# Hand-overs of a three-layer network on one core: norms' powers, weight splits, blanking and interleaving moved between engines and places

## The chip, the core and the metric

One core of one Trainium2 chip runs the whole program. The metric is device microseconds of one execution; a kernel's time is the median of its runs. TensorE (PE) does the matrix products, VectorE (DVE) and GpSimd (POOL) elementwise work, ScalarE (ACT) activations and copies, SyncE (SP) issues the transfers; PEld is PE's loading of stationary operands.

## The reference

A sequence of 512 tokens with 1024 features passes three residual layers, all in fp32: first a mixer (an RWKV-like scan beside a pooling branch) and the PEER layer, a lookup of 16 of 16384 experts in each of 8 heads; then a layer with an even mixer (latent and differential attention) and a gated convolutional FFN; then one with an odd mixer (dilated and stick-breaking attention) and another FFN. Around every mixer and FFN of the last two layers there are norms of this kind:

```python
def rms_norm(x, g):
    xf = x.astype(jnp.float32)
    y = xf * lax.rsqrt(jnp.mean(xf * xf, axis=-1, keepdims=True) + NORM_EPS)
    return (y * g.astype(jnp.float32)).astype(x.dtype)

h = conv_ffn(rms_norm(x, ffn_pre_g[i]), ffn_w_up[i], ffn_conv_w[i], ffn_conv_b[i], ffn_w_down[i])
x = x + rms_norm(h, ffn_post_g[i])
```

The first layer ends with one norm more (`norm_f`), whose output is the residual of what follows.

## The kernel before

**Products.** The 512 tokens are four tiles `t` of 128. Every fp32 product is made of three (`mm3`, lines 114 to 119): both operands are split into a rounded part and the rest, `hi` and `lo`, and hi·hi, hi·lo and lo·hi are summed in one PSUM bank. `K.unit` (58 to 68) fetches a weight tile of 128x1024 through the SP queue, lets ScalarE round it to `whi` (line 64) and subtracts to get `wlo` (line 67), on GpSimd and VectorE in turn unless an engine is named. The raw tile and each half have three buffers.

**Hand-overs.** At the end of a mixer or an FFN each token tile is normalised, added to the residual `st.x` and normalised again for the next layer. `square` (198) sums the squares of one half of 512 columns on ScalarE while it leaves PSUM; `add` (202) multiplies both halves by the gain on VectorE (208), calls `total`, and adds to the residual (211); `feed` (162) sums the squares of the new residual (169), calls `total`, and `lay` (179) scales by power and gain (185, VectorE), transposes on PE (190), copies to `hhi` (192, ScalarE) and subtracts to `hlo` (193, VectorE). `total` (173) adds the half sums and the epsilon on VectorE (176) and raises to -1/2 on GpSimd (177):

```python
nc.vector.scalar_tensor_tensor(out=r, in0=r, scalar=float(eps), in1=ms[:, 1:2], op0=ALU.add, op1=ALU.add)
nc.gpsimd.tensor_tensor(out=r, in0=r, in1=self.k.mhalf[:, 0:1], op=ALU.pow)
```

`Stream.project` (214) makes the next layer's first three units for columns 0 to 255 (tiles 0 and 1), then for the rest, so it starts once two tiles are laid. `project_out` (305) is a mixer's output projection for two token tiles; it is a generator that yields after each weight unit, and the last three units are taken tile by tile. `finished` (840) drives it and does the tile's hand-over when it is complete. In `ffn` (234) the last three units of the down projection are taken tile by tile as well; the first half of the output columns is kept in `y0` (287).

**The PEER end.** Tokens 0 to 127 do not go through the dense expert product: `chosen` (596) gathers their 256 expert rows by indirect transfers that GpSimd issues (619), with four row buffers, and VectorE folds each in (626, 635). The other 384 tokens meet all 128 expert units in `dense` (555): an up unit and a down unit each. `interleave` (2034) deals steps of a second generator between the steps of a first: after step i of `n_main` it has done `(i + 1) * n_fill // n_main`. Two gather steps go beside each of the first 26 dense units; from then on line 712 deals the rest, chained with `end` for tile 0, over 92 units. `end` (723) sums squares (735), yields, works out two powers on GpSimd (740 to 744) and lays the tile; for tile 0 the transposes are queued behind the last down matmul put down so far (`self.mark`), and they take the PSUM banks of the up products. Tiles 1 to 3 follow after the last down products.

**Order.** A scheduler orders each engine's instructions by readiness and by place in the program, so a later instruction can stand before an earlier one where nothing binds it. `issue_after` binds an instruction behind a given one on its engine. ScalarE evaluates its functions from loaded tables (ACT_TABLE_LOAD); `exp_ln` (70) loads the one that has both exp and ln.

**The odd mixer.** The query tiles are kept with one half of the partitions blank, so that two heads can share a key tile; `blank` (863) clears them on GpSimd before the first projection, and `apart` (856) fills the rest. In both mixers the last attention (`diff`, `dilated`) runs its token blocks 1 and 0, then blocks 3 and 2 with `finished` for tiles 0 and 1 in between, and then `finished` for tiles 2 and 3.

Of the kernel before, what the change touches and what calls it, by code (L numbers as in the profile page):

```python
# [135 lines left out]
class Stream:  # L136
# [25 lines left out]
    def feed(self, t, gain, pool):  # L162

        k, nc = self.k, self.k.nc
        ms = k.small.tile([128, 2], F32, name=k.name("ms"), tag="fms", bufs=4)
        y = pool.tile([128, D], F32, name=k.name("xn"), tag="xn", bufs=2)
        for h in range(2):
            sl = slice(h * 512, (h + 1) * 512)
            nc.scalar.activation(y[:, sl], self.x[:, t, sl], AF.Square, scale=1.0 / 32.0, accum_out=ms[:, h:h + 1])
        self.total(ms, 1e-6)  # L170
        self.lay(t, self.x[:, t, :], y, ms[:, 0:1], gain, lambda: self.bank("feed", (128, 4, 128)))

    def total(self, ms, eps):

        nc, r = self.k.nc, ms[:, 0:1]
        nc.vector.scalar_tensor_tensor(out=r, in0=r, scalar=float(eps), in1=ms[:, 1:2], op0=ALU.add, op1=ALU.add)
        nc.gpsimd.tensor_tensor(out=r, in0=r, in1=self.k.mhalf[:, 0:1], op=ALU.pow)

    def lay(self, t, x, y, r, gain, psum):

        k, nc = self.k, self.k.nc
        cols = slice(t * 128, (t + 1) * 128)
        for h in range(2):
            sl = slice(h * 512, (h + 1) * 512)
            nc.vector.scalar_tensor_tensor(out=y[:, sl], in0=x[:, sl], scalar=r, in1=gain[:, sl],  # L185
                                           op0=ALU.mult, op1=ALU.mult)
            p = psum()
            for i in range(4):
                c = 4 * h + i
                nc.tensor.transpose(p[:, i, :], y[:, c * 128:(c + 1) * 128], k.ident)  # L190
            hi, lo = self.hhi[:, 4 * h:4 * h + 4, cols], self.hlo[:, 4 * h:4 * h + 4, cols]
            nc.scalar.copy(hi, p)
            nc.vector.tensor_tensor(out=lo, in0=p, in1=hi, op=ALU.subtract)  # L193
# [8 lines left out]
    def add(self, t, halves, ms, gain, pool):  # L202
# [3 lines left out]
        cuts = [slice(h * 512, (h + 1) * 512) for h in range(2)]  # L206
        for h, sl in enumerate(cuts):
            V.tensor_tensor(out=y[:, sl], in0=halves[h], in1=gain[:, sl], op=ALU.mult)  # L208
        self.total(ms, 1e-6)
        for sl in cuts:  # L210
            V.scalar_tensor_tensor(out=self.x[:, t, sl], in0=y[:, sl], scalar=ms[:, 0:1], in1=self.x[:, t, sl],  # L211
# [22 lines left out]
def ffn(k, st, a, li, pre, out=None):  # L234
# [3 lines left out]
    with ExitStack() as ctx:  # L238
# [7 lines left out]
        with open_pool(tc, name=k.name("ffn_w"), bufs=2) as work:  # L246
# [10 lines left out]
            early = st.project([k.unit(a[f"ffn_up{li}"][i]) for i in range(3)], "up")  # L257
            for f in range(NF):
# [7 lines left out]
                V.tensor_tensor(out=alo[:, f, :], in0=us[0], in1=ahi[:, f, :], op=ALU.subtract)  # L266
        tail = ctx.enter_context(open_pool(tc, name=k.name("ffn_t"), bufs=1))
# [17 lines left out]
        for t in range(NT):  # L285
            st.square(acc[t], ms[t], 0, tail)
            A.copy(y0[:, t, :], acc[t])
# [6 lines left out]
        for t in range(NT):  # L294
# [3 lines left out]
            st.add(t, (y0[:, t, :], acc[t]), ms[t], gpost, tail)  # L298
# [6 lines left out]
def project_out(k, st, ohi, olo, w, toks):  # L305
# [9 lines left out]
    for c in range(n - 3):  # L315
        wt = k.unit(w[c])
# [3 lines left out]
    ws = [k.unit(w[c]) for c in range(n - 3, n)]  # L320
# [79 lines left out]
class Peer:  # L400
# [242 lines left out]
    def run(self, x, free_x, dram, ctx2, pre, ps, tag):  # L643
# [9 lines left out]
        with ExitStack() as ctx, ExitStack() as gctx, ExitStack() as ectx:  # L653
# [57 lines left out]
            with open_pool(tc, name="pe_gc", bufs=2) as self.gpool:  # L711
                interleave(dense, 118 - EARLY, chained(fill, self.end(st, 0, acc, g, gpre, tail, ps)), 258)
            rctx.close()
            run_all(self.last(gctx.enter_context(open_pool(tc, name="pe_last", bufs=1, side="right"))))
            tail = ctx.enter_context(open_pool(tc, name="pe_t2", bufs=2))
            for t in range(1, NT):
# [6 lines left out]
    def end(self, st, t, u, g, gpre, pool, ps):  # L723
# [13 lines left out]
        for _ in range(1 + 6 * (t == 0)):  # L737
            yield
        s = ms[:, :, 2]
        G.tensor_tensor(out=s, in0=ms[:, :, 0], in1=ms[:, :, 1], op=ALU.add)  # L740
        G.tensor_scalar(out=s[:, 0:1], in0=s[:, 0:1], scalar1=1e-5, scalar2=None, op0=ALU.add)
        G.tensor_scalar(out=ms[:, 0, 3:4], in0=s[:, 0:1], scalar1=1e-6, scalar2=None, op0=ALU.mult)
        G.tensor_tensor(out=s[:, 1:2], in0=s[:, 1:2], in1=ms[:, 0, 3:4], op=ALU.add)
        G.tensor_tensor(out=s, in0=s, in1=k.mhalf[:, 0:2], op=ALU.pow)
# [111 lines left out]
def apart(k, dst, src):  # L856


    k.nc.scalar.copy(dst[0][HALF[0]], src[HALF[0]])
    k.nc.vector.tensor_copy(dst[1][HALF[1]], src[HALF[1]])  # L860


def blank(k, pairs):
    for z in range(2):
        for pair in pairs:
            k.nc.gpsimd.memset(pair[z][HALF[1 - z]], 0.0)
# [6 lines left out]
def even(k, st, a, pre):  # L873
# [3 lines left out]
    with ExitStack() as ctx:  # L877
# [14 lines left out]
        k.exp_ln()  # L892
# [169 lines left out]
        run_all(at.pipeline([diff(h, i) for i in (1, 0) for h in range(4)], 2))  # L1062
        fill = finished(k, st, project_out(k, st, ohi, olo, wo, (0, 1)), gpost, gpre, tail)
        interleave(at.pipeline([diff(h, i) for i in (3, 2) for h in range(4)], 2), 8, fill, 14)
# [3 lines left out]
def odd(k, st, a, pre):  # L1068
# [3 lines left out]
    with ExitStack() as ctx:  # L1072
# [11 lines left out]
        blank(k, qs)  # L1084
        k.exp_ln()
# [3 lines left out]
        def proj(fs):  # L1089
            for f in fs:  # L1090
                p = st.project1(k.unit(a["od_in"][f]), "pj")
                if f < 6:
                    apart(k, qs[f], p)
# [24 lines left out]
        with open_pool(tc, name="od_st", bufs=2) as wk:  # L1118
# [48 lines left out]
            for y, p in zip((sq[0], sk[0], sq[1]), st.project([k.unit(a["od_in"][f]) for f in (12, 14, 13)], "lr")):  # L1167
                apart(k, y, p) if isinstance(y, list) else A.copy(y, p)
            A.copy(sk[1], st.project1(k.unit(a["od_in"][15]), "pj"))
# [55 lines left out]
        run_all(at.pipeline([dilated(hs, i) for i in (1, 0) for hs in (2, 3)], 2))  # L1225
        fill = finished(k, st, project_out(k, st, ohi, olo, wo, (0, 1)), gpost, gpre, tail)
        interleave(at.pipeline([dilated(hs, i) for i in (3, 2) for hs in (2, 3)], 2), 4, fill, 10)
# [932 lines left out]
```

## Time and profile before

| | |
|---|---|
| median of 3 runs | 3101.58 us (3099.12 to 3106.04) |
| the profiled execution's own time | 3105.84 us |
| its span, first to last instruction | 3104.1 us |
| mean granted clock of TensorE | 0.981 |
| PE, DVE, ACT, POOL busy | 95%, 65%, 44%, 25% |

The profile is of one execution. Times are microseconds from the start of its span, durations of groups nanoseconds. A row of a timeline gives start, duration, engine, line, operation, output and inputs by the program's names; in square brackets stands the idle time before it and what ended it. An engine that is held up inside an instruction shows as busy. The granted clock (PEclk) is TensorE's share of full speed, 1.00 for 2.4 GHz and 0.50 for 1.2.

### The profile page before, as it was taken

To read this page: it belongs to the slowest core of one execution; us is meant where nothing else is said; L and a number is where in the kernel's file an instruction comes from. 1 tells how busy PE (TensorE), PEld (TensorE's weight loads), DVE (VectorE), ACT (ScalarE), POOL (GpSimd) and SP (SyncE) were. 2 spreads that over 40 slices of the span, in tenths; PEclk is the share of its full clock that TensorE was granted. 3 is DMA by queue.
4 is the path that set the end of the run, shared out by engine and by line. 5 is a ranking of instruction groups with operands and counts; after the bars stand their busy time and mean duration, and the time that the engine had idled before them with its cause. 6 is when DMAs were issued, how large, how long until landed. Compare 5 with 4: busy or idle time off the path is not lost. (4 is left out here: it accounts for less than half of the span.)

```text
span 3104.1 us, 45731 instructions
## 1 busy us (share of the span) xinstructions
PE 2952.8 (95%) x17602; PEld 2493.7 (80%) x17602; DVE 2027.9 (65%) x3939; ACT 1359.3 (44%) x2483; POOL 768.8 (25%) x540
## 2 busy tenths in 40 slices
PE   7888999997899999999998999989999899999999
PEld 5666669997789999999997977668888777888887
DVE  6777668999987887888886446665551444655522
ACT  5444353357533333333333355564442354544422
POOL 0000015610014444444441022122222331122222
PEclk9999999999999999999999999899999999999999
DMA  2001152343348999999995432222332242133322
GB/s 91 27 20 33 62 182 97 102 147 153 146 151 315 335 331 345 321 337 336 332 336 210 140 101 82 89 96 96 99 98 94 79 136 91 52 100 99 95 95 82
DMA packets 176201, 476.07 MB, mean 153 GB/s; under 512 B 18768, under 2 KB 68688, under 8 KB 175728
## 3 DMA queue, kind: packets, MB, share of 16 engines
q1 hardware_dynamic: 139120, 338.93, 32.5%
q0 software_dynamic: 36864, 134.23, 11.8%
q8 instruction: 138, 2.26, 0.3%
q14 instruction: 79, 0.65, 0.1%
HBM read 448.59 MB, written 24.51 MB: 152 GB/s over the span
## 5 line engine op out<-in xcount | busy, mean ns | idle before, releaser
L64 ACT CAST whi<-raw 128x1024 fp32r<-128x1024 f32 x494 | 518.5, 1051 | 713.9 <-PE pu L118 190.7
L67 DVE TENSOR_TENSOR wlo<-raw,whi 128x1024 fp32r<-128x1024 f32 x366 | 457.6, 1251 | 462.4 <-ACT whi L64 453.6
L67 POOL TENSOR_TENSOR wlo<-raw,whi 128x1024 fp32r<-128x1024 f32 x128 | 310.8, 2430 | 1081.0 <-ACT whi L64 988.1
L117 PE MATMUL pu<-pe_hhi,whi 128*128 128x384 f32 x1024 | 349.6, 341 | 2.3 <-ACT gl L545 1.8
L119 PE MATMUL pu<-pe_hhi,wlo 128*128 128x384 f32 x1024 | 348.0, 340 | 0.0
L118 PE MATMUL pu<-pe_hlo,whi 128*128 128x384 f32 x1024 | 347.8, 340 | 0.0
L118 PE MATMUL pacc<-wlo,ahi 128*128 128x512 f32 x768 | 302.7, 395 | 0.0
L117 PE MATMUL pacc<-whi,ahi 128*128 128x512 f32 x768 | 294.1, 395 | 3.1 <-ACT ahi L590 3.1
L119 PE MATMUL pacc<-whi,alo 128*128 128x512 f32 x768 | 290.7, 398 | 3.3 <-DVE alo L591 3.3
L119 PE MATMUL up<-res_h,wlo 128*128 128x512 f32 (+1 forms) x752 | 283.1, 377 | 1.0 <-DVE wlo L67 1.0
L118 PE MATMUL up<-res_h,whi 128*128 128x512 f32 (+1 forms) x752 | 283.6, 377 | 0.0
L117 PE MATMUL up<-res_h,whi 128*128 128x512 f32 (+1 forms) x752 | 283.4, 378 | 0.1
L253 DVE SCALAR_TENSOR_TENSOR u<-up,ffn_par,u 128x511 f32<-128x511 f32 (+1 forms) x176 | 131.5, 748 | 142.8 <-ACT u L251 139.7
L619 POOL DMA_INDIRECT row<-pe_rows,pe_gs x128 | 166.0, 1297 | 195.9 <-DVE pe_gs L626 174.2
L619 POOL DMA_INDIRECT row<-pe_v,pe_gs x128 | 164.8, 1287 | 196.1 <-DVE pe_acc L635 186.0
L117 PEld LDWEIGHTS pu<-pe_hhi,whi 128*128 128x128 f32 x1024 | 193.4, 189 | 7.6 <-ACT gl L545 2.1
L118 PEld LDWEIGHTS pu<-pe_hlo,whi 128*128 128x128 f32 x1024 | 193.4, 189 | 4.1
L119 PEld LDWEIGHTS pu<-pe_hhi,wlo 128*128 128x128 f32 x1024 | 193.1, 189 | 0.5
L119 PEld LDWEIGHTS pacc<-whi,alo 128*128 128x128 f32 x768 | 145.0, 189 | 38.1 <-DVE alo L591 3.8
L117 PEld LDWEIGHTS pacc<-whi,ahi 128*128 128x128 f32 x768 | 144.3, 188 | 33.1 <-ACT ahi L590 3.8
L118 PEld LDWEIGHTS pacc<-wlo,ahi 128*128 128x128 f32 x768 | 144.3, 188 | 30.9
L635 DVE SCALAR_TENSOR_TENSOR pe_acc<-row,pe_gs,pe_acc 128x1024 f32<-128x1024 f32 x128 | 163.9, 1280 | 2.8 <-DMA row<-pe_v,pe_gs 2.3
(502 smaller groups left out, 6295.2 us busy)
## 6 DMA issues: line engine op xcount, KB each, us to landing
raw<-pe_u SPq DMA_DIRECT2D x128, 512.0 KB
raw<-pe_v SPq DMA_DIRECT2D x128, 512.0 KB
raw<-ffn_up SPq DMA_DIRECT2D x88, 512.0 KB
raw<-ffn_dn SPq DMA_DIRECT2D x44, 512.0 KB
pe_gd<-go SPq DMA_DIRECT2D x24, 784.0 KB
gc<-pe_gd SPq DMA_DIRECT2D x12, 1536.0 KB
mraw<-mx_in SPq DMA_DIRECT2D x80, 128.0 KB
raw<-pe_wq SPq DMA_DIRECT2D x16, 512.0 KB
```

The costliest lines, as they stand in the source:

```text
L64: nc.scalar.copy(hi, raw)
L67: eng.tensor_tensor(out=lo, in0=raw, in1=hi, op=ALU.subtract)
L117: mm(out, l[0], r[0], start=first, stop=False)
L118: mm(out, l[0], r[1], start=False, stop=False)
L119: return mm(out, l[1], r[0], start=False, stop=last)
L253: V.scalar_tensor_tensor(out=u[:, d:], in0=p[:, :S - d], scalar=par[:, o + 2 - d:o + 3 - d], in1=u[:, d:], op0=ALU.mult, op1=ALU.add)
L619: G.indirect_dma_start(out=r, out_offset=None, in_=table[z], in_offset=bass.IndirectOffsetOnAxis(ap=idx[:, j:j + 1], axis=0))
L635: V.scalar_tensor_tensor(out=acc, in0=row("v", j), scalar=w[:, j:j + 1], in1=acc, op0=ALU.mult, op1=ALU.add)
```

## The change

- `total` adds the epsilon to the first half's sum on VectorE, and ScalarE makes the power: Ln of the second sum with the first as bias, then Exp at scale -0.5. The tables for both are loaded after the FFN's up projection and after the last dense unit; the loads in `even` and `odd` go.
- `end` works out its sums on VectorE; for tiles 1 to 3 the power is Ln and Exp, for tile 0 it stays on GpSimd. Tile 0 yields 17 times before its power instead of 7, and 268 steps are dealt instead of 258.
- The weight splits of the FFN's first three units, of `project_out` and of the odd mixer's first four units are all on VectorE.
- In the FFN the first half of the output is multiplied by the gain on its way into `y0`, by VectorE, instead of copied by ScalarE.
- `apart` clears the blank halves on VectorE, queued behind the last `lo` of `lay`; `blank` goes.
- Four steps (in `odd` three) of `finished` are dealt into token blocks 1 and 0 of the last attention.

```diff
     def feed(self, t, gain, pool):
-        ms = k.small.tile([128, 2], F32, name=k.name("ms"), tag="fms", bufs=4)
+        ms = k.small.tile([128, 4], F32, name=k.name("ms"), tag="fms", bufs=4)
         for h in range(2):
-        self.total(ms, 1e-6)
-        self.lay(t, self.x[:, t, :], y, ms[:, 0:1], gain, lambda: self.bank("feed", (128, 4, 128)))
+        r = self.total(ms, 1e-6)
+        self.lay(t, self.x[:, t, :], y, r, gain, lambda: self.bank("feed", (128, 4, 128)))
     def total(self, ms, eps):
-        nc, r = self.k.nc, ms[:, 0:1]
-        nc.vector.scalar_tensor_tensor(out=r, in0=r, scalar=float(eps), in1=ms[:, 1:2], op0=ALU.add, op1=ALU.add)
-        nc.gpsimd.tensor_tensor(out=r, in0=r, in1=self.k.mhalf[:, 0:1], op=ALU.pow)
+        nc, r = self.k.nc, ms[:, 2:3]
+        nc.vector.tensor_scalar(out=ms[:, 0:1], in0=ms[:, 0:1], scalar1=float(eps), scalar2=None, op0=ALU.add)
+        nc.scalar.activation(r, ms[:, 1:2], AF.Ln, bias=ms[:, 0:1])
+        nc.scalar.activation(r, r, AF.Exp, scale=-0.5)
+        return r
     def lay(self, t, x, y, r, gain, psum):
...
-            nc.vector.tensor_tensor(out=lo, in0=p, in1=hi, op=ALU.subtract)
+            self.laid = nc.vector.tensor_tensor(out=lo, in0=p, in1=hi, op=ALU.subtract).ins
     def sums(self):
...
-    def add(self, t, halves, ms, gain, pool):
+    def add(self, t, halves, ms, gain, pool, y0=None):
+        ys = [y[:, sl] for sl in cuts]
+        if y0 is not None:
+            ys[0] = y0
         for h, sl in enumerate(cuts):
-            V.tensor_tensor(out=y[:, sl], in0=halves[h], in1=gain[:, sl], op=ALU.mult)
-        self.total(ms, 1e-6)
-        for sl in cuts:
-            V.scalar_tensor_tensor(out=self.x[:, t, sl], in0=y[:, sl], scalar=ms[:, 0:1], in1=self.x[:, t, sl],
+            if h or y0 is None:
+                V.tensor_tensor(out=ys[h], in0=halves[h], in1=gain[:, sl], op=ALU.mult)
+        r = self.total(ms, 1e-6)
+        for h, sl in enumerate(cuts):
+            V.scalar_tensor_tensor(out=self.x[:, t, sl], in0=ys[h], scalar=r, in1=self.x[:, t, sl],
     def project(self, units, bank):
...
-            early = st.project([k.unit(a[f"ffn_up{li}"][i]) for i in range(3)], "up")
+            early = st.project([k.unit(a[f"ffn_up{li}"][i], V) for i in range(3)], "up")
             for f in range(NF):
                 for i in (2 * f, 2 * f + 1):
...
+        k.exp_ln()
...
         for t in range(NT):
-            A.copy(y0[:, t, :], acc[t])
+            V.tensor_tensor(out=y0[:, t, :], in0=acc[t], in1=gpost[:, 0:512], op=ALU.mult)
         for f2 in range(n - 3):
...
             for i, w in enumerate(ws):
-            st.add(t, (y0[:, t, :], acc[t]), ms[t], gpost, tail)
+            st.add(t, (None, acc[t]), ms[t], gpost, tail, y0[:, t, :])
             if out is None:
...
     for c in range(n - 3):
-        wt = k.unit(w[c])
+        wt = k.unit(w[c], k.nc.vector)
         for t in toks:
-    ws = [k.unit(w[c]) for c in range(n - 3, n)]
+    ws = [k.unit(w[c], k.nc.vector) for c in range(n - 3, n)]
     for t in toks:
         for i, wt in enumerate(ws):
...
             for t in range(1, NT):
             with open_pool(tc, name="pe_gc", bufs=2) as self.gpool:
-                interleave(dense, 118 - EARLY, chained(fill, self.end(st, 0, acc, g, gpre, tail, ps)), 258)
+                interleave(dense, 118 - EARLY, chained(fill, self.end(st, 0, acc, g, gpre, tail, ps)), 268)
+            k.exp_ln()
             for t in range(1, NT):
...
             for z, src in ((0, u), (1, v)):
-        for _ in range(1 + 6 * (t == 0)):
+        for _ in range(1 + 16 * (t == 0)):
-        G.tensor_tensor(out=s, in0=ms[:, :, 0], in1=ms[:, :, 1], op=ALU.add)
-        G.tensor_scalar(out=s[:, 0:1], in0=s[:, 0:1], scalar1=1e-5, scalar2=None, op0=ALU.add)
-        G.tensor_scalar(out=ms[:, 0, 3:4], in0=s[:, 0:1], scalar1=1e-6, scalar2=None, op0=ALU.mult)
-        G.tensor_tensor(out=s[:, 1:2], in0=s[:, 1:2], in1=ms[:, 0, 3:4], op=ALU.add)
-        G.tensor_tensor(out=s, in0=s, in1=k.mhalf[:, 0:2], op=ALU.pow)
+        V.tensor_tensor(out=s, in0=ms[:, :, 0], in1=ms[:, :, 1], op=ALU.add)
+        V.tensor_scalar(out=s[:, 0:1], in0=s[:, 0:1], scalar1=1e-5, scalar2=None, op0=ALU.add)
+        V.scalar_tensor_tensor(out=s[:, 1:2], in0=s[:, 0:1], scalar=1e-6, in1=s[:, 1:2], op0=ALU.mult, op1=ALU.add)
+        if t:
+            A.activation(s, s, AF.Ln)
+            A.activation(s, s, AF.Exp, scale=-0.5)
+        else:
+            G.tensor_tensor(out=s, in0=s, in1=k.mhalf[:, 0:2], op=ALU.pow)
         with nullcontext() if t else k.tc.issue_after(self.mark):
...
-def apart(k, dst, src):
+def apart(k, st, dst, src):
+    with k.tc.issue_after(st.laid):
+        for z in range(2):
+            k.nc.vector.memset(dst[z][HALF[1 - z]], 0.0)
-def blank(k, pairs):
-    for z in range(2):
-        for pair in pairs:
-            k.nc.gpsimd.memset(pair[z][HALF[1 - z]], 0.0)
...
-        k.exp_ln()
...
-        run_all(at.pipeline([diff(h, i) for i in (1, 0) for h in range(4)], 2))
-        interleave(at.pipeline([diff(h, i) for i in (3, 2) for h in range(4)], 2), 8, fill, 14)
+        interleave(at.pipeline([diff(h, i) for i in (1, 0) for h in range(4)], 2), 8, itertools.islice(fill, 4), 4)
+        interleave(at.pipeline([diff(h, i) for i in (3, 2) for h in range(4)], 2), 8, fill, 10)
...
-        blank(k, qs)
-        k.exp_ln()
...
             for f in fs:
                 if f < 6:
-                    apart(k, qs[f], p)
+                    apart(k, st, qs[f], p)
...
-            for y, p in zip((sq[0], sk[0], sq[1]), st.project([k.unit(a["od_in"][f]) for f in (12, 14, 13)], "lr")):
-                apart(k, y, p) if isinstance(y, list) else A.copy(y, p)
-            A.copy(sk[1], st.project1(k.unit(a["od_in"][15]), "pj"))
+            for y, p in zip((sq[0], sk[0], sq[1]), st.project([k.unit(a["od_in"][f], V) for f in (12, 14, 13)], "lr")):
+                apart(k, st, y, p) if isinstance(y, list) else A.copy(y, p)
+            A.copy(sk[1], st.project1(k.unit(a["od_in"][15], V), "pj"))
...
-        run_all(at.pipeline([dilated(hs, i) for i in (1, 0) for hs in (2, 3)], 2))
-        interleave(at.pipeline([dilated(hs, i) for i in (3, 2) for hs in (2, 3)], 2), 4, fill, 10)
+        interleave(at.pipeline([dilated(hs, i) for i in (1, 0) for hs in (2, 3)], 2), 4, itertools.islice(fill, 3), 3)
+        interleave(at.pipeline([dilated(hs, i) for i in (3, 2) for hs in (2, 3)], 2), 4, fill, 7)
```

## Rows read from the trace of the kernel before

**Rows 1.** The page, part 1: busy us (share of the span) x instructions.

```profile
PE 2952.8 (95%) x17602; PEld 2493.7 (80%) x17602; DVE 2027.9 (65%) x3939; ACT 1359.3 (44%) x2483; POOL 768.8 (25%) x540
```

**Rows 2.** Stages: us; busy PE, PEld, DVE, ACT, POOL; PEclk, DMA, GB/s.

```profile
950.00:1650.00 700.00, 700.00 (x3488) 632.89 (x3488) 569.91 (x715) 248.32 (x340) 319.25 (x248) 1.00 0.94 337
```

**Rows 3.** Waits of PE from 1640 us: waited for, us, times, longest.

```profile
PE feed L190 <- DVE xn L185: 11.0, 3, 10.0
...
PE pf L190 <- DVE xn L185: 10.3, 1, 10.3
...
PE feed L190 <- DVE res_h L193: 5.5, 4, 2.1
...
PE lr L118 <- DVE res_h L193: 2.4, 1, 2.4
```

**Rows 4.** Busy time around the long waits, same columns as rows 2.

```profile
1668.20:1678.40 10.20, 0.00 (x0) 0.00 (x0) 6.39 (x8) 4.37 (x10) 1.57 (x5) 0.64 0.31 103
...
1678.40:1684.70 6.30, 5.71 (x20) 5.31 (x21) 2.04 (x3) 1.56 (x3) 0.00 (x0) 0.50 0.00 0
...
1985.00:2007.00 22.00, 18.91 (x62) 10.52 (x60) 14.45 (x70) 11.55 (x38) 2.77 (x2) 0.61 0.25 87
...
2452.30:2462.30 10.00, 0.00 (x0) 0.02 (x1) 10.00 (x12) 3.40 (x9) 7.23 (x10) 0.69 0.42 125
...
2462.30:2469.80 7.50, 6.36 (x28) 5.86 (x29) 6.54 (x12) 2.99 (x7) 2.04 (x3) 0.50 0.46 142
```

**Rows 5.** Timeline of DVE, 1666 to 1682 us: start, us, operation, idle before.

```profile
1670.42 2.60 DVE L635 SCALAR_TENSOR_TENSOR pe_acc<-row,pe_gs,pe_acc 128x1024 f32<-128x1024 f32 x2
...
1677.64 1.42 DVE L185 SCALAR_TENSOR_TENSOR xn<-v,ms,pe_gpre 128x512 f32<-128x512 f32 x2 [3.29 <-POOL ms L744]
```

**Rows 6.** Line 619 (the gathers): who waited for it.

```profile
  DVE row L626: 9.4, 11
```

**Rows 7.** Timeline of DVE, 2443 to 2464 us.

```profile
2451.56 1.73 DVE L176 SCALAR_TENSOR_TENSOR ms<-ms 128x1 f32<-128x1 f32 x1
...
2455.69 3.42 DVE L176 SCALAR_TENSOR_TENSOR pms<-pms 128x1 f32<-128x1 f32 x1
...
2461.43 1.40 DVE L185 SCALAR_TENSOR_TENSOR xn<-res_x,ms,pre 128x512 f32<-128x512 f32 x2
```

**Rows 8.** Timeline of POOL, 2443 to 2464 us.

```profile
2449.82 3.45 POOL L67 TENSOR_TENSOR wlo<-raw,whi 128x1024 fp32r<-128x1024 f32 x1 [0.30 <-POOL pms L177]
...
2453.33 2.96 POOL L866 MEMSET od_q<- 64x512 f32 x6
...
2456.76 2.33 POOL L67 TENSOR_TENSOR wlo<-raw,whi 128x1024 fp32r<-128x1024 f32 x1
```

**Rows 9.** Timeline of DVE, 3096 to 3101 us.

```profile
3097.69 0.69 DVE L208 TENSOR_TENSOR py<-ffn_y,post 128x512 f32<-128x512 f32 x1
...
3098.29 0.69 DVE L208 TENSOR_TENSOR py<-acc,post 128x512 f32<-128x512 f32 x1
```

**Rows 10.** Groups of line 67 from 1640 us: busy, mean ns | idle.

```profile
L67 POOL TENSOR_TENSOR wlo<-raw,whi 128x1024 fp32r<-128x1024 f32 x106 | 256.4, 2419 | 1036.6 <-ACT whi L64 943.7 <-issue 32.9 <-PE sp L785 16.9
...
L67 DVE TENSOR_TENSOR wlo<-raw,whi 128x1024 fp32r<-128x1024 f32 x141 | 177.8, 1261 | 359.4 <-ACT whi L64 356.0 <-PE pj L119 2.2 <-issue 0.9
```

**Rows 11.** Timeline of ACT, 1809 to 1814 us.

```profile
1809.45 1.28 ACT L893 ACT_TABLE_LOAD   x1
...
1810.75 0.20 ACT L893 ACTIVATE ev_ls<-ev_ls 128x2 f32<-128x2 f32 x1
...
1812.60 1.28 ACT L72 ACT_TABLE_LOAD   x1
```

**Rows 12.** Timeline of PE, 1982 to 1985 us.

```profile
1982.01 1.14 PE L117 MATMUL acc<-whi,ev_ohi 128*128 128x512 f32 x4
```

**Rows 13.** Timeline of ACT, 175 to 178 us.

```profile
174.99 1.28 ACT L1961 ACT_TABLE_LOAD   x1
...
176.99 1.28 ACT L1962 ACT_TABLE_LOAD   x1
```

## The prediction, as put on record before the run

> **What bounds the kernel now.** I read the page's busy table first, then the busy time by stage, then what TensorE (PE) waited for, then the granted clock around its long waits, then the instructions on either side of them. PE is busy for 95% of the span [rows 1]: it is the bound, and another engine counts only where PE stands still or runs at its lower level. The stretch from 950 to 1650 us is the dense part of the PEER layer: PE is busy for all of its 700 us at clock 1.00, beside DVE's 570 and DMA engines at a share of 0.94 [rows 2]. Nothing but less matrix work shortens that. What can be had lies in the hand-overs. After 1640 us the two longest waits of PE are both for a norm's result: 10.3 us for the gathered tile's `xn` (line 185) and 10.0 us in one wait for the same line at the end of the first FFN; next come 5.5 us in four pieces for `res_h` (line 193), at the end of the hand-overs [rows 3].
>
> A wait costs more than its length. From 1668.2 to 1678.4 PE does nothing and the granted clock falls; in the 6.3 us after it the clock is 0.50, so PE's 5.71 us there are work at 1.2 GHz that would take 2.85 at 2.4. After the second wait 6.36 us run at 0.50, 3.18 too many. In the even mixer's first attention blocks the mean clock is 0.61 without a long wait [rows 4].
>
> **The gathered tile** (`end` for t=0, line 712). Before, one fill step does one gathered row, and 258 steps are dealt over 92 dense units. The fill has 238 steps left when this begins (290 in all, 52 taken before); then come the sums, seven yields, and the step that lays the tile. The sums are therefore put down at 239·92/258 = 85.2, in the 86th unit, and the laying at 246·92/258 = 87.7, in the 88th. After: 239·92/268 = 82.0 and 256·92/268 = 87.9. So the transposes keep their place, behind the same mark, and what moves is the gathers, their sums and the norm's statistics: three units earlier. A unit is 42 matmuls; 3488 in 700 us [rows 2] make 8.4 us of it, so three are 25 us. Is there such a lead to be had? The last two rows are added from 1670.42 to 1673.02, and `xn` starts at 1677.64, after 3.29 us of waiting for GpSimd's power [rows 5]; PE is free at 1668.2. A lead of 25 us turns that lateness of 9.5 into slack. DVE waited for gathered data only 9.4 us in eleven pieces [rows 6]: its own order paces the gathers, and that order is what the edit advances. The SP queue is not touched; on GpSimd the 256 gathers go earlier, ahead of the power, which stays there for this tile. Gone: 10.3 idle, 0.6 behind it (6.30 less 5.71), 2.85 of slow clock [rows 3, 4], 13.7 in all. Left: the copy and the subtraction behind the transposes, whose banks the next unit takes, each near the 0.7 of a 128x512 row, of which the second half's transposes cover part; with a place in two queues I keep 1.7. **Term: 12.0, bounds 0 and 13.7.**
>
> **First FFN to odd mixer.** Between 2451 and 2461 us DVE is occupied but not working: a sum over 128x1 takes 1.73 us at 2451.56 and 3.42 at 2455.69, and `xn` of the second tile, for which PE waits, comes at 2461.43 [rows 7]. Those ends fall on the ends of two weight splits of GpSimd (3.45 from 2449.82, 2.33 from 2456.76); and between them six blanking memsets, 2.96 us, stand before the power that this `xn` needs [rows 8]. The change takes all three off GpSimd: the power goes to ScalarE as two activations on 128x1, the four `od_in` splits to DVE, the twelve memsets behind the last laying on DVE. In the same order `xn` gains 1.58 + 3.27 (the sums at their usual 0.15) and three multiplications by the gain, 0.6 from one start to the next [rows 9], that now stand in the FFN's middle, and loses two splits at 1.23 to 1.26 [rows 10]: 4.85 + 1.8 - 2.5 = 4.2 us. On ScalarE an activation on 128x2 takes 0.20 [rows 11]; four per tile come to 0.8 us, and ScalarE is idle for 6.6 of the gap's 10.0 [rows 4]. The gap shrinks to about six and its slow tail by part: 4.2 + 2.3 (of 1.1 more waiting, 7.50 less 6.36, and 3.2 of clock). **Term: 6.5, bounds 2 and 12**: 2 if the splits all stand before `xn`, 12 if the order closes up. The memsets, at POOL's 0.49 each 5.9 us, lie where DVE has room; were that gone they would hold up the score stage by as much.
>
> **The other hand-overs.** Even mixer to FFN and odd mixer to FFN: the same removal of GpSimd against two more DVE splits each (1.26 against 2.42, rows 10). PE's longest wait for `res_h`, 2.1 us, is of this kind [rows 3] and comes once in each. **1.5 each, bounds -2.5 (both splits in PE's way) and 4.** Tiles 1 to 3 of the PEER end: five GpSimd steps become three small DVE ones and two activations; the wait at hand is 2.4 [rows 3]. **1.5, bounds 0 and 2.4, with its clock 4.** The last tile: one multiplication of 0.6 less between the last sum and the output [rows 9]. **0.6, bounds 0 and 0.7.** Copies of `y0` that become multiplications sit between FFN halves: 0, since PE has the next weights ready; without that cover 4 x 0.7.
>
> **The interleaving in the mixers.** Four (odd: three) steps of `project_out` are dealt into the first attention blocks. Bounds: -4 if the projection's splits, all on DVE now, come before scores, and 8, half of PE's slow time at 1985 to 2007 [rows 4], if the extra matmuls lift the clock. I take 0: the scheduler already places matmuls of `project_out` at 1982, ahead of these blocks [rows 12], so the order in the source says little there. Its weight loads on the SP queue are as many as before and already issued that early.
>
> **Sum.** 12.0 + 6.5 + 1.5 + 1.5 + 1.5 + 0.6 = 23.6. The profiled execution took 3105.84 (span 3104.1), 4.3 above the median of 3101.58. Against it: 3082.2; on the median: 3078.0. Hereafter a difference under 0.2%, 6.2 us, counts as none, as a measurement of this kernel could not tell it.
>
> **Rivals.** (a) *The gathered tile stays late.* If gathers are paced by their own round trip (GpSimd issues a row when DVE frees a buffer) and not by the order, an earlier place gains about 1 instead of 12: 3089. For: DMA share 0.94 [rows 2]. Against: rows 6. Chance 0.15. (b) *Clocks too.* If the attention blocks and every hand-over stay at 2.4 GHz, add 8 and 6: 3064. For: 0.61 in rows 4. Chance 0.08. (c) *DVE becomes the bound.* The calls changed concern 34 units, of which about 17 leave GpSimd; 17 x 1.26 = 21.4 us all in PE's way [rows 10] leave 3099, no change. Against: in the gaps DVE is stalled more than loaded [rows 7]. Chance 0.08. (d) *Tables, the slower side.* Ln and Exp load two different tables unless the joint one stands before them: in the mixer each pair costs two loads of 1.28 us [rows 13], and before the even mixer the joint load (line 72) came after the Exp it was meant for, which fetched its own [rows 11]. The new kernel has 31 pairs; if the preload falls behind or is undone, each costs 2.56 on ScalarE. With five pairs in the way at each of three hand-overs, three at the PEER end and one at the last tile, 19 x 2.56 = 48.6: 3127. It decides from 9 pairs on (23.6/2.56). Against: in the FFNs the preload stands ahead of the whole down projection, and three loads leave the hand-overs. Chance 0.05, and 0.02 for other slowing.
>
> The Trainium skill, page "ScalarE: Activation LUTs", section "What ACT_TABLE_LOAD costs", gives about 2.66 us for each switch of set, so (d) would by it give 3179. The rows show the load at 1.28 and the next activation 0.02 later [rows 11], and the sum goes by them.
>
> **How the numbers follow.** The forecast has 0.62; with (a) and (b) faster has 0.85. (c) and a little else make 0.09 for no change, (d) and the rest 0.06 for slower. The terms' bounds, not all at one end, make some 10 us either way for the forecast alone (3068 to 3088); down to 3064 takes in (b), up to 3094 takes in (a): 8 in 10.
>
> **What would show it.** Right: PE's wait at 1668 under 2.5 us and no half clock after it; `xn` of the second tile before 2457 on the old scale; GpSimd without line-177 powers and with some 89 splits after 1640 instead of 106; one table load per hand-over block, between units and not between tiles; no DVE sum over 0.3 us. Wrong: loads at Ln lines; PE gaps in 950 to 1650; new waits of PE for `wlo` or for scores.

## The result, and the profile after

The changed kernel takes 3130.76 us (median of 4 runs, 3128.36 to 3138.68), the kernel before 3103.16 (its three earlier runs and one more): a ratio of 1.0091, 95% interval 1.0076 to 1.0106. It is slower by 28 us where 23.6 less were forecast, outside the range, and near the 3127 of the rival with the tables.

First the page's busy table and what PE waited for after 1640 us (what it waited for; us in total, number of waits, longest), in the changed kernel:

```profile
PE 2961.3 (95%) x17602; PEld 2501.1 (80%) x17602; DVE 2042.8 (65%) x3985; ACT 1408.4 (45%) x2572; POOL 693.4 (22%) x463
```

```profile
PE pf L192 <- DVE xn L187: 15.3, 3, 9.7
PE feed L192 <- DVE xn L187: 11.6, 3, 5.2
PE tp L816 <- ACT rstd L846: 6.6, 3, 4.4
...
PE feed L192 <- DVE res_h L195: 6.2, 2, 5.1
PE tp L844 <- ACT rsq L843: 3.4, 3, 2.6
```

PE's busy time hardly moved [rows 1]. The wait for the gathered tile's `xn`, 10.3 us in [rows 3], still stands at 9.7; the one at the first FFN's end has gone from 10.0 to 5.1; and there are new ones for ScalarE's results inside the even mixer.

To see where the time went, both traces are cut at events that both have. The first column below is the start of the first down product; then come five stretches: to the end of the last up product (it holds the gathered tile); from there to the first matmul of the even mixer (the PEER end); to the first conversion of the first FFN, that is, ScalarE's first `u<-up` (the even mixer and its hand-over); to the first matmul of the odd mixer (the FFN and its hand-over); to the first conversion of the second FFN (the odd mixer and its hand-over); to the last output. The first 811 us, which no edit touches, differ by up to 5 us between executions, and the dense part by 1 to 3; the even mixer can differ by 6 (below), the others by 0.7 at most. One execution of each kernel; the labels are those of the experiments, and (2) is a second execution.

```
                     start   dense   PEER   even    FFN     odd    FFN
                     at      part    end    mixer   and end mixer  and end
before               811.5   976.9   16.4   296.5   362.7   282.7   353.9
changed              809.2   976.4   25.1   323.0   357.9   279.7   353.5
t1                   811.8   974.7   18.6   290.6   357.7   280.0   353.5
t2                   812.2   978.2   25.2   293.3   358.0   279.8   353.5
p0                   812.6   977.0   16.5   286.6   358.6   276.9   354.1
p0 (2)               812.2   976.8   16.5   286.5   358.6   276.8   354.1
c1                   811.1   975.6   19.1   300.2   361.4   282.3   353.4
c2                   811.3   976.5   16.4   285.9   358.9   275.9   353.9
b2                   814.0   975.6   16.5   291.5   358.6   276.5   354.1
b2 (2)               811.1   977.1   16.5   285.0   358.6   277.2   354.1
b3                   810.2   976.2   16.5   297.0   360.1   281.5   354.1
b4                   809.1   976.2   16.5   286.5   358.6   276.3   354.1
g1                   809.9   966.4   16.4   300.6   362.5   282.1   353.9
g1 (2)               811.1   967.8   16.4   301.4   362.5   282.2   353.9
b1                   809.7   966.7   16.5   286.3   358.0   277.1   354.1
c3                   812.5   962.1   19.0   297.4   358.0   280.3   353.5
c3 (2)               810.2   965.4   19.1   291.3   358.0   280.6   353.5
c4                   811.1   965.7   16.5   287.0   356.0   278.9   354.1
d1                   809.2   966.7   16.4   286.4   358.3   275.5   354.0
```

The loss lies in two neighbours: 8.7 us at the PEER end and 26.5 in the even mixer. Behind them the changed kernel is faster, by 4.8, 3.0 and 0.4. The next rows say what fills the two stretches: the groups of table loads from 1780 to 2140 us of the changed kernel (where the kernel before had three loads in the same stretch), and the timeline of ScalarE at the end of the dense part.

```profile
L177 ACT ACT_TABLE_LOAD x8 | 10.3, 1283 | 0.1
...
L178 ACT ACT_TABLE_LOAD x7 | 9.0, 1283 | 0.1
...
L846 ACT ACT_TABLE_LOAD x6 | 7.7, 1283 | 0.1
L847 ACT ACT_TABLE_LOAD x6 | 7.7, 1283 | 0.1
...
L752 ACT ACT_TABLE_LOAD x3 | 3.8, 1283 | 0.1
L753 ACT ACT_TABLE_LOAD x3 | 3.8, 1283 | 0.1
...
L804 ACT ACT_TABLE_LOAD x1 | 1.3, 1283 | 0.0
```

```profile
1781.31 1.05 ACT L64 CAST whi<-raw 128x1024 fp32r<-128x1024 f32 x1 [3.02 <-PE pu L118]
1782.38 1.28 ACT L72 ACT_TABLE_LOAD   x1
1783.66 1.28 ACT L552 ACT_TABLE_LOAD   x1
1784.96 0.49 ACT L552 ACTIVATE gl<-pu 128x384 f32<-128x384 f32 x1
...
1801.52 1.28 ACT L752 ACT_TABLE_LOAD   x1
...
1804.58 1.28 ACT L753 ACT_TABLE_LOAD   x1
1805.88 0.21 ACT L753 ACTIVATE ms<-ms 128x2 f32<-128x2 f32 x1
```

The joint table is loaded at 1782.38, and the very next instruction is a Gelu, whose own load throws it out at 1783.66. From then on every Ln and every Exp loads its own table: 34 loads of 1.28 us before the first FFN's Silu. The preload is traced after the dense part and pinned behind the instruction traced last on ScalarE, a weight's cast (1781.31); nothing pins the last Gelu, traced earlier, ahead of it, and it was set behind. PE pays inside the even mixer, where Ln and Exp of the attention's own norm alternate with those of the hand-over (timelines of ScalarE and of PE):

```profile
2063.94 1.28 ACT L178 ACT_TABLE_LOAD   x1
...
2066.07 1.28 ACT L846 ACT_TABLE_LOAD   x1
2067.36 0.69 ACT L846 ACTIVATE rstd<-tp,eps 128x512 f32<-128x512 f32 x1
```

```profile
2061.66 2.08 PE L844 MATMUL tp<-rsq,ev_ones 128*128 128x512 f32 x2 [2.57 <-ACT rsq L843]
2068.11 0.90 PE L816 MATMUL tp<-ident,s 128*128 128x128 f32 x3 [4.37 <-ACT rstd L846]
```

### The profile page after: what moved, and what is told of

It reads as the page before. It is cut to its first block, busy times and chain, and to the rows that moved or that the text cites. A ratio compares the mean times of both kernels' runs of the same rounds, so it can differ in the third digit from the quotient of the medians.

```text
span 3128.3 us, 45779 instructions
## 1 busy us (share of the span) xinstructions
PE 2961.3 (95%) x17602; PEld 2501.1 (80%) x17602; DVE 2042.8 (65%) x3985; ACT 1408.4 (45%) x2572; POOL 693.4 (22%) x463
## 4 chain that ended last, share of the span: by engine, by line
PE 77%; DVE 9%; ACT 4%; issue 1%; DMA 1%; POOL 1%; DVEq 0%; SPq 0%; ACTq 0%; POOLq 0%
PE pacc L119 6%; PE pacc L117 6%; PE pacc L118 6%; PE pu L117 5%; PE pu L119 5%; PE pu L118 5%; PE up L117 5%; PE up L118 5%; PE up L119 5%; PE acc L117 3%; PE acc L118 3%; PE acc L119 3%; PE pj L117 2%; PE pj L118 2%; PE pj L119 2%; PE sp L796 2%
## 5 line engine op out<-in xcount | busy, mean ns | idle before, releaser
L67 DVE TENSOR_TENSOR wlo<-raw,whi 128x1024 fp32r<-128x1024 f32 x384 | 475.3, 1239 | 440.9 <-ACT whi L64 431.2
L67 POOL TENSOR_TENSOR wlo<-raw,whi 128x1024 fp32r<-128x1024 f32 x110 | 266.6, 2426 | 1245.6 <-ACT whi L64 1217.0
L119 PE MATMUL pu<-pe_hhi,wlo 128*128 128x384 f32 x1024 | 348.1, 340 | 0.0
L119 PE MATMUL pacc<-whi,alo 128*128 128x512 f32 x768 | 291.3, 398 | 3.3 <-DVE alo L598 3.3
```

The lines of the kernel that those rows point to most:

```text
L67: eng.tensor_tensor(out=lo, in0=raw, in1=hi, op=ALU.subtract)
L119: return mm(out, l[1], r[0], start=False, stop=last)
```

## The experiments

The ratio of an experiment is to runs of the kernel before that were made beside it (medians 3103.92 to 3106.34). Profiles are of one execution each, which need not be the median one.

**Tables: t1 and t2.** t1 loads the table behind the last Gelu, t2 only puts back the even mixer's load.

```diff
 t1, in dense, behind the up unit of i
+            if i == 127:
+                k.exp_ln()
 t1, in run
-            k.exp_ln()
 t2, in even
+        k.exp_ln()
         A.activation(ls[:, 0:2], ls[:, 0:2], AF.Exp)
```

> The changed kernel with the joint table's load traced right behind the last Gelu of the dense part, so that no Gelu follows it. Tables theory: the 34 loads between 1801 and 2124 us go, and with them the 31 us by which the first FFN's first Silu load fell behind (2105.7 before, 2136.7 after): 3094 to 3104 us, and no load between the PEER end and the first FFN's Silu. Rival (the splits moved to VectorE and the steps dealt into the first attention blocks are what costs): the loads lie beside other work, and it stays above 3120.

> The changed kernel with the even mixer's joint load put back where it was and nothing else. Tables theory: the six loads of tiles 1 to 3 at the PEER end stay and cost the 8.7 us that were lost there (3.0 us ahead at 1676, 6.0 behind at the first projection), the other 28 go with some 22 us: about 3108, 3104 to 3113. Rival (splits and dealt steps): above 3120.

t1: 3090.44 us, ratio 0.996 (0.9946 to 0.9973). t2: 3098.75, 0.9981 (0.9971 to 0.9992). So the tables are the loss, and all of it. From the last up product to the first conversion the changed kernel took 348.1 us and t1 309.2: 38.9 us for 33 loads more, 1.18 each. That is near a load's 1.28, but it is not all waiting. The two stretches in the changed kernel and in t1 (us; busy PE, PEld, DVE, ACT, POOL; PEclk, DMA, GB/s):

```profile
1785.70:2133.75 348.05, 301.03 (x1461) 234.36 (x1460) 188.22 (x441) 225.48 (x444) 33.71 (x15) 0.89 0.25 81
```

```profile
1786.55:2095.75 309.20, 286.89 (x1464) 224.07 (x1463) 185.43 (x439) 181.93 (x410) 33.75 (x15) 0.95 0.29 92
```

PE stands idle for 47.0 us in the one and 22.3 in the other: 24.7 us of waiting, 0.75 a load. The other 14.1 us are PE's own work, the same matmuls at a granted clock of 0.89 instead of 0.95; some 6 of them can be the difference between executions. t1 came out 3.6 us below its range and t2 5 us below. Both ranges took off the 31 us by which the changed kernel fell behind, from which the hand-overs' gains were already deducted. In t2, which keeps the PEER end's six loads and its 25.2 us, 6.6 over t1, the even mixer's 28 loads gave back 29.7 us (323.0 to 293.3) where 22 were counted, though the profiled execution, 3105.21, was the slowest of twelve. The load's row in t1, the only one between the last Gelu and the Silu:

```profile
1787.89 1.28 ACT L72 ACT_TABLE_LOAD   x1
```

**Gathered tile: g1 and b1.** Six more yields in each case move the transposes past two more dense units: g1 in the kernel before, b1 in p0 (below).

```diff
 g1
-        for _ in range(1 + 6 * (t == 0)):
+        for _ in range(1 + 12 * (t == 0)):
 b1
-        for _ in range(1 + 16 * (t == 0)):
+        for _ in range(1 + 22 * (t == 0)):
```

> The kernel before with 13 yields in place of 7 for tile 0 and the total of 258 kept: the gathers' folds keep their place in VectorE's queue, the transposes go two dense units (16.8 us) later. Queue-order theory (folds are ordered by the scheduler's readiness, not by their place in the program, so only the transposes can be moved): PE's wait of 10.3 us for xn is gone with its slow clock, 3103 - 13 = 3090, 3087 to 3094. Rival (the transposes take the banks of the up products and stall the next unit wherever they stand): a wait of 3 us or more in another place, 3096 to 3103.

> The changed kernel with the power on GpSimd (3086.7) and 23 yields in place of 17 for tile 0, so that its transposes stand two dense units later. Queue-order theory: PE's wait of 9.7 us for xn goes, 2.1 stay behind the transposes for their banks, the slow clock goes too: 10 us less up to the last up product, as in the kernel before (976.9 to 966.4), and 3077 if the even mixer keeps its time; 3081 if it is put in another order that costs the 4 us seen there. Rival (the even mixer gives all of it back): 3085 or more.

g1: 3099.17 us, 0.998 (0.9969 to 0.9991). b1: 3076.74, 0.9915 (0.9898 to 0.9932). The timelines of VectorE show why the change gained nothing here, and that of PE in b1 what a later place does:

```profile
1668.08 2.60 DVE L642 SCALAR_TENSOR_TENSOR pe_acc<-row,pe_gs,pe_acc 128x1024 f32<-128x1024 f32 x2
...
1674.71 1.41 DVE L187 SCALAR_TENSOR_TENSOR xn<-v,ms,pe_gpre 128x512 f32<-128x512 f32 x2 [0.85 <-POOL ms L755]
```

```profile
1685.98 0.69 PE L117 MATMUL pu<-pe_hhi,whi 128*128 128x384 f32 x1 [2.12 <-DVE res_h L194]
```

In the changed kernel the last two rows are folded in 2.3 us before the place of [rows 5], and the whole dense part began 2.3 us earlier too (809.2 against 811.5): nothing moved but `xn`, by 0.6. The order in the traces says the same: the first 2768 instructions of VectorE, all folds of the gathers among them, stand in the same order in both kernels, by operation and tile. With the transposes two units later PE waits only the 2.1 us in which the banks come free, and the dense part is 10.5 and 10.3 us shorter. In g1 the even mixer took 4 to 5 us longer than in the kernel before, in both executions, and gave half of the gain back. So g1 missed its range (3087 to 3094) and has the number of its rival, but not the rival's reason: no wait of PE between 1640 and 1800 us is over 2.5. In b1 the even mixer gave nothing back.

**Power and splits, undone and alone: p0, c1, b3, c2.** p0 is the changed kernel with the power on GpSimd, b3 is p0 with the splits in turn. c1 is the kernel before with the power on ScalarE alone (with `end`'s sums on VectorE and t1's preload), c2 with the 34 splits on VectorE alone.

```diff
 p0 against the changed kernel (loads as before; `end` likewise)
...
-        nc.scalar.activation(r, ms[:, 1:2], AF.Ln, bias=ms[:, 0:1])
-        nc.scalar.activation(r, r, AF.Exp, scale=-0.5)
+        nc.gpsimd.tensor_tensor(out=r, in0=r, in1=self.k.mhalf[:, 0:1], op=ALU.pow)
 c2 against the kernel before (b3 the other way)
-        wt = k.unit(w[c])
+        wt = k.unit(w[c], k.nc.vector)
...
```

> The changed kernel with the norms' power left on GpSimd and the joint loads where the kernel before has them; splits, blanking, y0 by multiplication, the dealt steps and the 17 yields stay. Tables theory: the loss goes with the power, 3094 to 3104. Rival (splits and dealt steps): it stays above 3115.

> The kernel before with nothing but the power as Ln and Exp on ScalarE, its table loaded behind the last Gelu and after each up projection. Queue theory (the pair stands in ScalarE's queue behind casts and squares and takes longer from sum to use than GpSimd did): the PEER end goes from 16.4 to 18.6, the mixers' hand-overs gain nothing, only the first FFN's end gains some 3 us as the memsets no longer stand before the power: 3100 to 3106. Rival (the forecast's view: ScalarE is idle there, the power costs 0.4 per norm): 3090 to 3096.

> The changed kernel with the power on GpSimd and the splits of the FFN's first units, of the mixers' projections and of the odd mixer's first units in turn on GpSimd and VectorE again. Theory that the splits held GpSimd's power and VectorE's small sums: the hand-overs go back, 4 us at the first FFN's end, 7 at the odd mixer's, 5 at the even one's, 3097 to 3103, and sums on VectorE of over 1 us come back. Rival (blanking, y0 and dealt steps made the gain): 3085 to 3090.

> The kernel before with nothing but the 34 splits on VectorE. Theory (the splits on GpSimd held up VectorE's operations with two SBUF inputs): first hand-over of the even mixer to the first FFN conversion 52.0 to 47.0, the same at the odd mixer 39.7 to 32.7, the first FFN's end 1.5 to 4 less, the even mixer unchanged at 221 as no steps are dealt: 3087 to 3091. Rival (the forecast's: a split on VectorE costs it 1.26 in the way, which eats most of the gain): 3097 to 3102.

p0: 3086.69 us, 0.9941 (0.9927 to 0.9956). c1: 3106.29, 1.0006 (0.9996 to 1.0017). b3: 3099.9, 0.9986 (0.9974 to 0.9997). c2: 3083.39, 0.9936 (0.9921 to 0.9951). The splits alone gain 21.6 us; the power alone gains nothing, and beside the splits it costs 4 (t1 against p0). p0 and c2 came out 7 and 4 us below their ranges, c1 0.3 above. With the splits in turn the rest of the change still gains some 4 us (b3), more than half of it in the first FFN and its end (360.1 against 362.7).

Of c2's 10.6 us in the even mixer 4.9 lie behind the first transpose of its hand-over (52.0 to 47.1). The other 5.7 lie ahead of it, where neither the forecast nor c2's expectation ("unchanged at 221") looked for a gain: in all five executions with the splits in turn that part takes 244.5 us or more, in eight of the nine with the splits on VectorE and the power on GpSimd 239.6 or less. The kernel before, then c2 (columns as above):

```profile
1804.84:2049.34 244.50, 231.58 (x1135) 177.76 (x1136) 144.72 (x366) 141.96 (x313) 52.45 (x31) 0.94 0.26 86
```

```profile
1804.19:2042.95 238.76, 226.72 (x1137) 175.34 (x1137) 143.97 (x367) 142.50 (x314) 37.11 (x24) 0.96 0.28 88
```

PE is idle there about as long (12.9 and 12.0 us) and works 4.9 us less, at a higher granted clock. How the splits bring that about was not found out.

In the hand-overs one place shows what splits and power do, the odd mixer's hand-over, first in the kernel before (VectorE, GpSimd), then in p0 (VectorE, GpSimd), then in t1 (VectorE, ScalarE):

```profile
2727.98 3.56 DVE L211 SCALAR_TENSOR_TENSOR res_x<-py,pms,res_x 128x512 f32<-128x512 f32 x2 [0.58 <-POOL pms L177]
...
2728.42 2.57 POOL L67 TENSOR_TENSOR wlo<-raw,whi 128x1024 fp32r<-128x1024 f32 x1
```

```profile
2711.68 0.36 DVE L176 SCALAR_TENSOR_TENSOR pms<-pms 128x1 f32<-128x1 f32 x2
2712.49 1.42 DVE L216 SCALAR_TENSOR_TENSOR res_x<-py,pms,res_x 128x512 f32<-128x512 f32 x2 [0.44 <-POOL pms L177]
...
2711.91 1.04 POOL L177 TENSOR_TENSOR pms<-pms,mhalf 128x1 f32<-128x1 f32 x2 [15.02 <-DVE pms L176]
```

```profile
2714.35 0.14 DVE L176 TENSOR_SCALAR pms<-pms 128x1 f32<-128x1 f32 x1
...
2717.37 1.41 DVE L217 SCALAR_TENSOR_TENSOR res_x<-py,pms,res_x 128x512 f32<-128x512 f32 x2
...
2714.52 0.60 ACT L202 ACTIVATE pj<-acc 128x512 f32<-128x512 f32 x1
...
2715.14 1.05 ACT L64 CAST whi<-raw 128x1024 fp32r<-128x1024 f32 x1
2716.10 0.48 ACT L177 ACTIVATE pms<-pms 128x1 f32<-128x1 f32 x2
2716.48 0.33 ACT L178 ACTIVATE pms<-pms 128x1 f32<-128x1 f32 x2
```

Before, two additions took 3.56 us, to 0.6 behind the end of GpSimd's split (2730.99). (The Trainium skill, "SBUF — State Buffer", "Who interferes with whom", has VectorE's second pair of ports shared with GpSimd under an exclusive lock; these rows agree.) From 1804 us on VectorE's additions of line 211 and its sums of line 176 are occupied for 38.2 us before and 27.2 in c2. In p0 the two additions take 1.42 and start 0.8 us after the sum (2711.68), by way of GpSimd, which has nothing else to do there. In t1 the sum starts at 2714.35, but Ln stands behind a squaring and a cast in ScalarE's queue and Exp behind two Ln; the additions, by then behind a split too, start at 2717.37, 3.0 later.

**Dealt steps and blanking: b2 and b4**, each p0 with one part undone.

```diff
 b2, in even (in odd likewise)
-        interleave(at.pipeline([diff(h, i) for i in (1, 0) for h in range(4)], 2), 8, itertools.islice(fill, 4), 4)
+        run_all(at.pipeline([diff(h, i) for i in (1, 0) for h in range(4)], 2))
 b4, in odd
+                k.nc.gpsimd.memset(pair[z][HALF[1 - z]], 0.0)
...
```

> The changed kernel with the power on GpSimd, and the steps of the projection no longer dealt into token blocks 1 and 0. Theory that dealing gained in the mixers: the even mixer from its first unit to its first hand-over goes from 215.9 back to about 221, 3092. Rival (the gain there came with the splits on VectorE): 216 stays, 3087.

> The changed kernel with the power on GpSimd and the twelve blanking memsets on GpSimd at the odd mixer's start again. Theory that they stood before the power: six of 2.96 us together delay xn of the second tile, the wait at the first FFN's end grows from 6.0 to 8 or 9 and its slow clock with it, 3089 to 3092. Rival (with no split on GpSimd they find room): no change, 3085 to 3088, or 1 to 2 us less since VectorE has twelve operations fewer.

b2: 3084.11 us, 0.9931 (0.9916 to 0.9945). b4: 3082.05, 0.9927 (0.9912 to 0.9942). Neither is slower than p0, and both lie below the numbers expected of theory and rival. With these splits off GpSimd the memsets find room: the FFN's stretch is 358.6 in p0 and b4. Of the 5.6 us between the profiled executions of p0 and b4, 4.3 lie in the first 811 us and the dense part, which its edit doesn't reach. Only b2's even mixer was 4.9 us longer, as g1's and c3's (below) were beside the kernels they come from. Second executions were to tell whether the order of the attention blocks or the execution made that:

> A second profiled execution of the changed kernel with the power on GpSimd. Order theory: from the first matmul of the even mixer to the first conversion of the FFN it takes 286.6 again, within 1. Execution theory: any value from 286 to 292.

> A second profiled execution of that kernel without the dealt steps. Order theory: 291.5 again, within 1. Execution theory: nearer to 286.5, as the first one was the slowest of its six runs.

> A second profiled execution of the kernel before with later transposes. Order theory: 300.6 again, within 1. Execution theory: nearer to the 296.5 of the kernel before.

> A second profiled execution of the kernel with both slips mended. Order theory: 297.4 again, within 1. Execution theory: nearer to the 290.6 of the run that mended the tables alone.

One execution each: 3087.16, 3085.21, 3100.78 and 3083.2 us. p0 repeats to 0.1 and g1 to 0.8; b2 falls from 291.5 to 285.0, c3 from 297.4 to 291.3. So in b2 and c3 it was the execution, and dealing the steps gains nothing. PE runs the same 1138 instructions in the same order from the even mixer's first to its first transpose in both executions of b2, and the whole difference comes in 40 of them. These 40 in b2's first and second execution (columns as above):

```profile
1998.40:2017.40 19.00, 17.87 (x41) 8.72 (x41) 11.18 (x45) 10.38 (x31) 0.00 (x0) 0.50 0.00 0
```

```profile
1997.50:2009.80 12.30, 10.96 (x42) 5.33 (x42) 9.45 (x39) 9.59 (x30) 0.00 (x0) 1.00 0.00 1
```

PE waits about as little in both (1.1 and 1.3 us); the granted clock is 0.50 in the one and 1.00 in the other.

**Both slips mended, and beyond: c3, c4, d1.** c3 is the change with both slips mended (t1 with 23 yields). c4 is b1 with two of the odd mixer's splits behind the first tile's last subtraction (`laid0`). d1 is the kernel before with c2's and g1's edits, six lines.

```diff
 c4
+            us = [k.unit(a["od_in"][12], V)]
+            with tc.issue_after(st.laid0):
+                us += [k.unit(a["od_in"][f], V) for f in (14, 13)]
...
```

> The changed kernel with its table loaded behind the last Gelu and with 23 yields in place of 17, that is, with the transposes two units later: what the forecast took the change to be. By the two runs that mended one of them each: 3090.4 - 10.4 = 3080, 3076 to 3084. Rival (the even mixer falls into another order and gives the gain back, as in the run on the kernel before): 3086 or more.

> The run with later transposes and the power on GpSimd (3076.7), with two of the odd mixer's first three splits queued on VectorE behind the first tile's last lo instead of before the second tile's xn. Theory (those two, 1.2 us each, are what PE's 6.0 us at the first FFN's end consist of besides the norm itself): the wait goes to 3.5 to 4.5 and the stretch from the first conversion to the odd mixer's first unit from 358.0 to about 355.5: 3073 to 3076. Rival (the third tile becomes late instead, or the split is late for PE): the same total time, the wait in another place.

> The kernel before with the 34 splits on VectorE and tile 0's transposes two units later, and nothing else. Theory that these two are all that gains (splits 3105 to 3083.4, transposes 10.4 up to the last up product): 3073, 3070 to 3077, and level with the run that also has the dealt steps, the y0 products and the blanking moved (3076.7). Rival (dealt steps, y0 or blanking gain beside them, or the even mixer falls into a slower order): 3079 or more.

c3: 3086.03 us, 0.9946 (0.9929 to 0.9963): above its range, at the rival's number, but not for the rival's reason alone: the dense part gained 9 to 13, the even mixer gave 6.8 of it back in one execution and 0.7 in the other. What its median would be without that was not separated. c4: 3074.94, 0.9908 (0.9891 to 0.9925), inside its range but no different from b1, as its rival had it: the wait of 6.0 became 4.1 and the FFN's stretch 2.0 shorter, another wait grew behind it, and the odd mixer's stretch is 1.8 longer (timeline of PE):

```profile
2434.63 1.85 PE L191 MATMUL feed<-ident,xn 128*128 128x128 f32 x8 [4.10 <-DVE res_h L194]
...
2439.49 0.58 PE L118 MATMUL lr<-res_h,whi 128*128 128x256 f32 x1 [2.17 <-DVE res_h L194]
```

d1: 3072.79 us, 0.9906 (0.989 to 0.9922), level with b1 and c4 and 58 below the changed kernel. The splits and the later transposes are the gain; beside them the rest of the change adds nothing.

## Why the prediction was wrong

**Tables.** The step that failed is the argument against rival (d): that the preload stands ahead where it matters. That is so in the FFNs, and there it held (one load before each second half, none within). But the PEER end and the even mixer hung on one preload whose place nothing ensured, and [rows 11] showed the pattern: an Exp that fetched its own table 3.15 us before the load meant for it. Rival (d), which had 48.6 us for 38 loads, was given 0.05; the runs show 38.9 for 33. Its price per load came out near for a reason it did not have: 24.7 us are waiting and 14.1 a lower clock. The Trainium skill's 2.66 us a switch ("ScalarE: Activation LUTs", "What ACT_TABLE_LOAD costs") would make 33 switches 88 us, an estimate, and more than twice what was lost; the next activation starts 0.02 after the load's end here too (1804.58 and 1805.88). The same page ("Table sets: the hidden batching unit") counts one load for ln followed by exp, as one set has both; here each loaded its own until the joint one was loaded by name.

**The gathered tile, 12.0.** The step "that order is what the edit advances" failed. The deal sets the place in the program; the folds' order in VectorE's queue stayed as it was. (That the scheduler went by readiness fits, but no run separates it from other causes.) Only the transposes are bound to a place, and 246 of 258 and 256 of 268 put them into the same unit. Measured: 0.6. Once they really moved, 10.3 to 10.5 came, inside the bounds of 0 and 13.7, with 2.1 left for the banks where 1.7 had been kept. Rival (a), 0.15, had the right result; its reason, the gathers' own round trip, was not tested, since the order never moved.

**The hand-overs.** First FFN to odd mixer: 6.5 forecast, 5.0 in t1. Even mixer to FFN and odd mixer to FFN, 1.5 each: 3.4 (52.0 to 48.6 from the first transpose to the first conversion) and 2.7 in t1, within the bounds; in p0 5.0 and, for the odd mixer as a whole, 5.8. The splits' price was too high: c2 shows that on VectorE they don't stand in PE's way but take the place of longer holds. The power's was too low: 0.8 us a tile counted its instructions and not its place in ScalarE's queue. So the PEER end, 1.5 forecast, lost 2.2 in t1, whose one load there holds up nothing: ScalarE is idle for 1.2 us behind it. The last tile's 0.6 was 0.4. The dealt steps' 0 stands, and so does that of the first halves kept as products: the FFN takes 358.3 in d1, which copies them, and 358.0 in b1.

With (a) granted, the terms left 3089 to 3090; t1, where only the tables are mended, has 3090.44. That is partly luck. The PEER end and the first FFN's end fell short by 3.7 and 1.5; the mixers' hand-overs gave 3.1 more than forecast, the even mixer ahead of its hand-over 2.5 that no term has, and the dense part 2.2 that lie within the spread of executions. The two slips that were rivals both came true; their sum would have been 3138. Of the signs named, loads at Ln lines came, as did GpSimd's fewer splits (88 after 1640 us, 89 forecast).

## What to carry to other kernels

A preload that nothing but the trace's order holds must be pinned behind the last use of the old table, not behind whatever was traced before it; its proof is the list of loads in the order of the engine's queue, next to the last activation that needs the old table. A deal of steps moves only what is bound to a place: ask of each step what orders it. And a short operation moved to an engine whose queue is occupied at that moment costs its wait in that queue; an idle engine can be the nearer one.

## What was not expected of the hardware

33 loads of 1.28 us cost 1.18 us each of the kernel's time although ScalarE was busy for only 45% of the span: 0.75 us as waits of PE, the rest as PE's work at a lower granted clock. And TensorE's clock decided a stretch without a single long wait: b2's even mixer took 291.5 us in one execution and 285.0 in another, with the same matmuls in the same order, 40 of them at a granted clock of 0.50 in the one and 1.00 in the other. In g1 the stretch was longer in both executions. What makes the clock fall in one execution and not in the other was not found out.
